# Layer 0 of a two-layer block: the first granule finished and normalized once, and the q/k/v epilogues begun one by one behind their last sums

## The chip, the core and the metric

One Trainium2 chip, one of its cores. The metric is the device time of one execution in microseconds (us). Engines are named as in the profile: PE is TensorE, DVE is VectorE, ACT is ScalarE, POOL is GpSimd, and SP is the queue that issues most DMAs. Each engine works off its own instructions strictly in the order in which the program wrote them; a waiting instruction holds up all that stand behind it on its engine.

## The reference

Two layers on x of 256 tokens by 2048 features, all in float32. Each layer computes six adaLN vectors from the condition c, a mixer (layer 0: differential attention; layer 1: an SSD scan) and a SwiGLU. What bears on the change is the start of layer 0:

```python
ada = silu(c) @ ada_w[0] + ada_b[0]              # shift1, scale1, gate1, shift2, scale2, gate2
h = rms_norm(x, norm1_g[0]) * (1.0 + scale1) + shift1
q, k, v = split(h @ da_w_in)                     # 2048 columns each: 16 heads of 2 x 64 (v: 128)
q = partial_rope(rms_norm(q, q_norm_g)); k = partial_rope(rms_norm(k, k_norm_g))
a = softmax(q0 k0) - lam * softmax(q1 k1)        # causal, two softmaxes for each head
x = x + gate1 * (rms_norm(a @ v, subln_g) * (1 - lambda_init)) @ w_out
```

## The kernel before

**Matrix products.** Weights arrive by DMA in units of 256 rows by 512 columns (a tile `raw`, one of 7). ACT rounds a unit to the fast format (`wh`, the "cast" of line 253), DVE makes the rest (`wl` = raw - wh), and PE multiplies three times (high by high, high by low, low by high): 12 matmuls of 512 columns for one unit and 256 tokens. At most four units are split ahead of their products (`W_BUFS`), so the cast of a unit is written into ACT's queue when the products of the fourth unit before it are written into PE's. A unit's `wl` is written one unit later than its cast.

**Order.** The program is one stream: units go into a list (`fifo`) together with plain calls (`call(fn)`), and are popped from it in turn. Popping writes instructions into the engines' queues. Generators in `active` (epilogues, attention blocks) are advanced one step after each popped unit (`step_all`, by `tick`).

**Granules.** shift1 and scale1 are needed before h exists, and their weights (`ada_first`, tiles `araw`, 9 buffers) have to be loaded as well. So the start is cut into eight granules g of 256 features. `push_mods(g)` multiplies the eight `araw` units of a granule in pairs ("adaLN pairs", 8 matmuls of 32 output rows, tile `po` or `wk`); `finishes[g]` turns the sums into columns T0 and S0 (four small matmuls `wk<-c,adasb` on PE, three short DVE operations T, S, S); `normed(g)` makes h of the granule (`hm`, then `ah` and `al`). Then `push_early(n, g)` multiplies this granule with six chunks of 512 columns, n = 0 to 5. By their names in `keys` they are q0, k0, v0, q1, k1, v1 (the q, k and v columns of head groups 0 and 1). Its `collect` copies (g = 0, ACT) or adds (g > 0, DVE) the two PSUM banks of the unit to an SBUF pair `part[n]`, called `partoh` (even n) and `partol` (odd n) in the profile. There are four such banks (`mm`), so the second unit after one waits for that one's sum.

The function `item(i, g)` places the work of granule g-1 among the eight `araw` units i of granule g. For g = 1 it finishes and normalizes granule 0 at i = 0, before its first products; and the two branches `elif i == 1` and `elif i == 2`, which hold for every g from 1 on, do both a second time for g = 1.

**Epilogues.** After the sums of granule 7, `complete(n, ...)` starts the end of a chunk: v is copied (line 989), q and k run `epilogue`, at most three at a time (`EPI`): squares on ACT (924), sums of 64 on DVE (`qss`), 1/sqrt on POOL (388, 389: one pair for each half b of the tokens), 16 scalings of 64 columns on ACT (937), the rotation on POOL and DVE, transposes on PE into a `wk` bank (three of these), and ACT's evacuation of each bank to `qT` or `kT` (959). Attention blocks (`attend`) of a head group start when its q and k are done: products of q and k on PE (`wk<-negm,identb`, then `wk<-kT,qT`), maxima on DVE, exponentials on ACT (1031), the combination of the two softmaxes on DVE (tile `e`), transposes of e on PE, their copy on ACT, products with v.

**The chunks after.** From n = 6 on (q2, k2, ...) each chunk is one product over all 2048 rows, 8 units in a row in one pair of `mm` banks; the first six epilogues and the first attention blocks run beside chunk 6. Adds of adaLN rows (`acc`) for later stages run on DVE in between.

Of the kernel before, what the change touches and what calls it, by code (L numbers as in the profile page):

```python
# [90 lines left out]
def block_kernel(ctx: ExitStack, tc: tile.TileContext, x, x_t, columns_in, ssd_columns, da_columns, ada_w, ada_b,  # L91
# [85 lines left out]
    def step_all():  # L177
        for g in list(active):
            if next(g, StopIteration) is StopIteration:
                active.remove(g)  # L180
        gap["n"] -= 1
        if pending and gap["n"] <= 0 and pending[0][0]():
            _, g, n = pending.popleft()
            gap["n"] = n
            if next(g, StopIteration) is not StopIteration:
                active.append(g)
# [40 lines left out]
    def pop():  # L227
        kind, fn = fifo.popleft()
        if kind == "c":
            fn()  # L230
            return
        if waiting["u"] <= 1:
            low_parts()
        done = fn()
        waiting[kind] -= 1 if done is None else done
        if kind == "u":
            tick()

    def flush():
        low_parts()  # L240
        while fifo:
            pop()

    def call(fn):
        fifo.append(("c", fn))
# [17 lines left out]
    def push_unit(w, row, col, n, mm):  # L263
        while waiting["u"] >= limit["u"]:
            pop()
        u = split_unit(w, row, col, n)
        waiting["u"] += 1
        fifo.append(("u", lambda: mm(u)))
# [10 lines left out]
    def products(ps, hl, half, w, n, first, last):  # L279
        h, l = hl  # L280
        wh, wl = w
        for a in range(2):
            k = 2 * half + a
            pe.matmul(ps[:, :n], h[:, k, :], wh[:, a, :n], start=first and a == 0, stop=False)
            pe.matmul(ps[:, :n], h[:, k, :], wl[:, a, :n], start=False, stop=False)
            pe.matmul(ps[:, :n], l[:, k, :], wh[:, a, :n], start=False, stop=last and a == 1)
# [458 lines left out]
    def small_loads():  # L745
        sp.dma_start(da_cols, da_columns[:, 0:36])
        sp.dma_start(lv, da_columns[:, 36:292].rearrange("p (i d) -> p i d", i=4))
# [75 lines left out]
    def push_mods(g, item):  # L823

        st = {}
        sl = slice(2 * g, 2 * g + 2)

        def use(raw, u):
            if u == 0:
                st["ps"] = bank(("po", "wk")[g % 2])  # L830
            if u % 2 == 0:
                st["raw"] = raw
                return
            for k in range(2 * u - 2, 2 * u + 2):
                t = k % 4
                pe.matmul(st["ps"][32 * t:32 * t + 32, :], cT32[:, k, :], (st["raw"], raw)[t // 2][:, k % 2, :],
                          start=(k < 4), stop=(k >= 12), tile_position=(0, 32 * t), skip_group_check=True)
            if u == 7:
                st["sb"] = tmp("adasb")
                act.copy(st["sb"], st["ps"])  # L840

        def finish():
            ps2 = bank("wk")
            for i in range(4):
                pe.matmul(ps2[:, i:i + 1], st["sb"][:, i * 128:(i + 1) * 128], c32, start=True, stop=True)
            dve.tensor_tensor(T0[:, sl], ps2[:, 0:2], b_cols[0, 0][:, sl], op=ALU.add)
            dve.tensor_tensor(S0[:, sl], ps2[:, 2:4], b_cols[0, 1][:, sl], op=ALU.add)
            dve.scalar_tensor_tensor(S0[:, sl], S0[:, sl], 1.0, n1c[0][:, sl], op0=ALU.add, op1=ALU.mult)
        for u in range(8):
            item(u)  # L850
            push_raw(ada_first, u * 256, g * 512, lambda raw, u=u: use(raw, u), first)
        return finish
# [39 lines left out]
    def scale_quarter(q):  # L892
        v = x_quarter(q).rearrange("p (k t) -> p k t", k=4)
        dve.tensor_tensor(v, v, held["rps"][:, None, 0:256].to_broadcast([128, 4, 256]), op=ALU.mult)
# [18 lines left out]
    n_early = N_EARLY  # L913
    part = {}
# [50 lines left out]
    def complete(n, src, in_psum):  # L965

        hg, i = keys[n]
        nm = ("q", "k", "v")[i]

        def ahead():  # L970
            return hg >= 2 and (begun, ended)[i == 2][hg - 2] < 3
        if in_psum:
            while ahead():
                step_all()
            if i < 2:
                tiles = []
                for b in range(2):
                    t = held["dp"].tile([128, 512], F32, tag="qn", name="qn", bufs=2)
                    act.copy(t, src[b])
                    tiles.append(t)  # L980
                src = tiles

        def steps(src=src):
            while ahead():
                yield
            if i == 2:
                v = held["dp"].tile([128, 2, 512], F32, tag="v", name="v", bufs=2)
                for b in range(2):
                    act.copy(v[:, b, :], src[b])
                ready[n] = v  # L990
            else:
                dst = held["dp"].tile([128, 4, 256], F32, tag=f"{nm}T", name=f"{nm}T", bufs=2)
                yield from epilogue(nm, dst, n, src)
        g = steps()
        if next(g, StopIteration) is not StopIteration:
            active.append(g)
# [117 lines left out]
    def push_early(n, g):  # L1114

        hg, i = keys[n]
        q, half = g // 2, g % 2
        bk = Banks()

        def run(u):  # L1120
            for b in range(2):
                products(bk()[b], norm_a.h[q][b], half, u, 512, True, True)
        push_unit(wi, g * 256, i * D + hg * 512, 512, run)

        def collect():
            if g == 0:
                tg = ("oh", "ol")[n % 2]
                part[n] = [op_.tile([128, 4, 128], F32, tag=tg, name=f"part{tg}")
                           .rearrange("p a n -> p (a n)") for b in range(2)]
            for b in range(2):  # L1130
                if g == 0:
                    act.copy(part[n][b], bk()[b])
                else:
                    dve.tensor_tensor(part[n][b], part[n][b], bk()[b], op=ALU.add)
        call(collect)

    ada_job(0, 2, fin_gate("m0", True), gate=True)
# [16 lines left out]
    def normed(g):  # L1154
        norm_pair(g)
        done.append(g)

    def item(i, g):
        if g == 0:
            if i in (2, 6):  # L1160
                call(token_rstd if i == 2 else scale_tokens)
            return
        at["p"] += 1
        first = 0 if g == 1 else 3
        if g == 1 and i == 0:
            flush()
            for fn in (finishes[0], low_parts, lambda: normed(0)):
                call(fn)
            push_early(0, 0)
            small_loads()  # L1170
            dve.tensor_copy(identb, ident)
        elif i == 1:
            call(finishes[g - 1])
        elif i == 2:
            call(lambda: normed(g - 1))
        if g == 1 and i in (3, 5, 7):
            call(lambda: scale_quarter(i // 2))
        if i == first:
            while g - 1 not in done:
                pop()  # L1180
            todo.extend((n, g - 1) for n in range(1 if g == 1 else 0, n_early))
            lead = 2 if g == 1 else 0
            span.update({"from": at["p"] - lead, "to": at["p"] + 8 - lead, "n": len(todo)})
        while todo and len(todo) * (span["to"] - span["from"]) > span["n"] * (span["to"] - at["p"]):
            push_early(*todo.popleft())

    for g in range(8):
        if g == 2:
            call(lambda: active.append(rotary_tables()))
        if g == 4:  # L1190
            call(lambda: ada.update(rate=1.5, metered=METER))
        finishes.append(push_mods(g, lambda i, g=g: item(i, g)))
    for k in range(max(3, len(todo))):
        if k == 1:
            call(finishes[7])
        elif k == 2:
            call(lambda: norm_pair(7))
            call(open_dp)
        if todo:
            push_early(*todo.popleft())  # L1200
    call(lambda: ada.update(rate=0.0, acc=0.0))
    for n in range(n_early):
        push_early(n, 7)
    call(lambda: [complete(n, part[n], False) for n in range(n_early)])
    call(lambda: ada.update(rate=DA_RATE, metered=METER))

    def load_x():
# [3 lines left out]
    for n in range(n_early, 12):  # L1211
        if n == n_early + 1:
            call(load_x)
        hg, i = keys[n]
# [649 lines left out]
```

## Time and profile before

| | |
|---|---|
| time, median of 3 runs | 2683.26 us (2683.25 to 2684.19) |
| the profiled execution | 2684.56 us, of which the trace's span is 2682.8 us |
| PE busy | 2637.8 us (98% of the span) |
| DVE busy | 1956.5 us (73%) |
| ACT busy | 1373.9 us (51%) |
| DMA | mean 255 GB/s |

The profile is of one execution. Times in its rows count from the start of the span. Shares over the whole span are averages over stages; what the changed lines are worth is read from the first 300 us, where they work.

### The profile page before, as it was taken

How to read it: one execution, taken by the hardware profiler on the slowest of the kernel's cores; microseconds unless marked ns; L12 is line 12 of the kernel's file. 1: busy time of each engine (PE TensorE's matmuls, PEld its weight loads, DVE VectorE, ACT ScalarE, POOL GpSimd, SP SyncE). 2: the span in 40 equal slices, each digit the busy share in tenths (PEclk: the TensorE clock that was granted, in tenths of full speed). 3: DMA queues.
4: the chain of work that ended last, by engine and by line, in shares of the span. 5: the costliest groups of instructions: out<-in, count | busy, mean ns of one | idle time of the engine just before them, and what ended most of it. 6: DMA issues, size and time to landing. Idle time of an engine off the chain costs nothing.

```text
span 2682.8 us, 35840 instructions
## 1 busy us (share of the span) xinstructions
PE 2637.8 (98%) x13224; PEld 2191.7 (82%) x13224; DVE 1956.5 (73%) x2240; ACT 1373.9 (51%) x2037; POOL 197.7 (7%) x205
## 2 busy tenths in 40 slices
PE   7997999999999999999999999999999999999999
PEld 4665887888888888888999989988888888888887
DVE  4876887777888876777777777786677554446776
ACT  4336775545444444446546566565545444444443
POOL 0003331000111210001000010000000000000001
PEclk9998999999999999999999999999999999999999
DMA  8985787698889887885566666666687655556885
GB/s 348 373 308 194 255 282 291 233 346 305 308 310 345 317 316 254 287 290 179 169 229 227 214 233 234 206 234 193 201 316 287 191 185 188 193 188 229 284 287 184
DMA packets 193136, 685.09 MB, mean 255 GB/s; under 512 B 22224, under 2 KB 30784, under 8 KB 191680
## 3 DMA queue, kind: packets, MB, share of 16 engines
q1 hardware_dynamic: 191232, 680.93, 72.4%
q8 instruction: 104, 1.70, 0.3%
q0 software_dynamic: 864, 1.62, 0.2%
q14 instruction: 72, 0.59, 0.1%
q10 hardware_dynamic: 864, 0.24, 0.0%
HBM read 680.52 MB, written 2.19 MB: 254 GB/s over the span
## 4 chain that ended last, share of the span: by engine, by line
PE 94%; DVE 2%; ACT 2%; DMA 1%; issue 1%; POOL 1%; SPq 0%; DVEq 0%; ACTq 0%; POOLq 0%
PE mm L118 75%; PE wk L118 15%; PE po L118 4%; DMA araw<-in_ada_w 1%; DVE wl L118 1%; ACT wh L253 0%; POOL qr L389 0%; DMA raw<-in_da_w_in 0%; DVE res L118 0%; DVE x L118 0%; ACT partol L937 0%; ACT e L1031 0%; DVE acc L118 0%; DVE partol L118 0%; ACT hm L554 0%
## 5 line engine op out<-in xcount | busy, mean ns | idle before, releaser
L253 ACT CAST wh<-raw 128x1024 fp32r<-128x1024 f32 (+1 forms) x888 | 924.5, 1046 | 1071.4 <-PE mm L118 776.9
L118 DVE TENSOR_TENSOR wl<-raw,wh 128x1024 fp32r<-128x1024 f32 (+1 forms) x888 | 1104.4, 1253 | 442.0 <-ACT wh L253 438.6
L118 PE MATMUL mm<-wh,ah 128*128 128x512 f32 (+1 forms) x2560 | 1017.9, 398 | 8.0 <-ACT ah L907 3.8
L118 PE MATMUL mm<-wl,ah 128*128 128x512 f32 (+1 forms) x2560 | 1000.0, 391 | 4.0 <-DVE wl L118 4.0
L118 PE MATMUL mm<-wh,al 128*128 128x512 f32 (+1 forms) x2560 | 1000.3, 391 | 0.0
L118 PEld LDWEIGHTS mm<-wh,ah 128*128 128x128 f32 x2560 | 482.6, 189 | 131.2 <-issue 18.7
L118 PEld LDWEIGHTS mm<-wl,ah 128*128 128x128 f32 x2560 | 483.0, 189 | 104.1 <-DVE wl L118 7.1
L118 PEld LDWEIGHTS mm<-wh,al 128*128 128x128 f32 x2560 | 482.3, 188 | 103.3 <-DVE al L118 1.9
L118 DVE SCALAR_TENSOR_TENSOR acc<-raw,cT,acc 128x1024 f32<-128x1024 f32 x300 | 383.4, 1278 | 0.3
L118 PE MATMUL wk<-wl,ah 128*128 128x512 f32 x360 | 140.2, 389 | 0.0
L118 PE MATMUL wk<-wh,ah 128*128 128x512 f32 x360 | 140.1, 389 | 0.0
L118 PE MATMUL wk<-wh,al 128*128 128x512 f32 x360 | 140.0, 389 | 0.0
L118 PE MATMUL mm<-ah,wh 128*128 128x256 f32 x720 | 118.8, 285 | 0.0
L118 PE MATMUL mm<-al,wh 128*128 128x256 f32 x720 | 117.7, 283 | 0.0
L118 PE MATMUL mm<-ah,wl 128*128 128x256 f32 x720 | 117.6, 283 | 0.0
L508 POOL PARTITION_ALL_REDUCE gate<-acc x12 | 41.2, 3477 | 943.2 <-DVE acc L118 936.4
L118 PEld LDWEIGHTS mm<-ah,wh 128*128 128x128 f32 x720 | 100.2, 192 | 0.1
L118 PEld LDWEIGHTS mm<-ah,wl 128*128 128x128 f32 x720 | 100.2, 192 | 0.0
L118 PEld LDWEIGHTS mm<-al,wh 128*128 128x128 f32 x720 | 100.2, 192 | 0.0
L118 PEld LDWEIGHTS wk<-wl,ah 128*128 128x128 f32 x360 | 67.5, 188 | 14.2 <-DVE wl L118 0.4
L118 PEld LDWEIGHTS wk<-wh,al 128*128 128x128 f32 x360 | 67.6, 188 | 14.1
L118 PEld LDWEIGHTS wk<-wh,ah 128*128 128x128 f32 x360 | 67.6, 188 | 14.1
(305 smaller groups left out, 2047.8 us busy)
## 6 DMA issues: line engine op xcount, KB each, us to landing
raw<-in_ffn_w_gate_up SPq DMA_DIRECT2D x352, 512.0 KB, 4.6
raw<-in_ada_w SPq DMA_DIRECT2D x320, 512.0 KB, 5.1
raw<-in_ffn_w_down SPq DMA_DIRECT2D x176, 512.0 KB, 4.8
raw<-in_ssd_w_in SPq DMA_DIRECT2D x136, 512.0 KB, 4.5
raw<-in_da_w_in SPq DMA_DIRECT2D x96, 512.0 KB, 5.3
araw<-in_ada_w SPq DMA_DIRECT2D x64, 512.0 KB, 8.4
raw<-in_ssd_w_out SPq DMA_DIRECT2D x64, 512.0 KB, 4.3
raw<-in_da_w_out SPq DMA_DIRECT2D x32, 512.0 KB, 5.4
```

The source lines that it names most:

```text
L118: return fn(dst, *a, **k)
L253: act.copy(wh[:, :, :n], raw[:, :, :n])
L508: pool.partition_all_reduce(mods["G", key][:, o:o + 512], acc[:, i * 512:(i + 1) * 512], 128, ReduceOp.add)
```

## The change

`item` leaves out the second finish and the second normalization of granule 0. `complete` is no longer called for all six chunks in one go behind the last sum of granule 7, but for each chunk behind its own last sum.

```diff
@@ push_early, collect @@
                     act.copy(part[n][b], bk()[b])
                 else:
                     dve.tensor_tensor(part[n][b], part[n][b], bk()[b], op=ALU.add)
+            if g == 7:
+                complete(n, part[n], False)
         call(collect)
@@ item @@
-        elif i == 1:
+        elif i == 1 and g > 1:
             call(finishes[g - 1])
-        elif i == 2:
+        elif i == 2 and g > 1:
             call(lambda: normed(g - 1))
@@ behind the granules @@
     for n in range(n_early):
         push_early(n, 7)
-    call(lambda: [complete(n, part[n], False) for n in range(n_early)])
     call(lambda: ada.update(rate=DA_RATE, metered=METER))
```

How the queues change is shown at three places. The first is PE's queue behind the third of granule 0's six products (36 matmuls `mm`), a piece of the difference, where `wk<-c,adasb` are the small matmuls of the finish and `wk<-araw,cT` is the first adaLN pair of granule 1:

```order
 L118 MATMUL mm<-wl,ah 128x512
 L118 MATMUL mm<-wh,al 128x512
-L118 MATMUL wk<-c_96,adasb 128x1 x4
 L118 MATMUL wk<-araw,cT_115 32x512 x4
 L118 MATMUL mm<-wh,ah 128x512
```

The four small matmuls are gone; on ACT and DVE the second `hm`, `ah` and T, S, S, `al` are gone in the same way, and everything else stands in the same order there.

The second place is ACT's queue from the casts behind the last normalization (granule 7) on. Before, the third of these seven casts is that of v1's last unit, and the seventh that of the fourth unit of chunk 6:

```order
L253 CAST wh<-raw 128x1024 x7
L924 ACTIVATE sq<-partoh 128x512 x2
L924 ACTIVATE sq<-partol 128x512 x2
L989 COPY v<-partoh 128x512 x2
L924 ACTIVATE sq<-partol 128x512 x2
L989 COPY v<-partol 128x512 x2
L253 CAST wh<-raw 128x1024 x2
L937 ACTIVATE partoh<-partoh,qr 128x64 x8
L937 ACTIVATE partol<-partol,qr 128x64 x16
L253 CAST wh<-raw 128x1024
L937 ACTIVATE partoh<-partoh,qr 128x64 x8
L937 ACTIVATE partol<-partol,qr 128x64 x16
```

and now, in the same queue from the same place:

```order
L253 CAST wh<-raw 128x1024 x2
L924 ACTIVATE sq<-partoh 128x512 x2
L253 CAST wh<-raw 128x1024
L924 ACTIVATE sq<-partol 128x512 x2
L253 CAST wh<-raw 128x1024
L989 COPY v<-partoh 128x512 x2
L937 ACTIVATE partoh<-partoh,qr 128x64 x8
L253 CAST wh<-raw 128x1024
L924 ACTIVATE sq<-partol 128x512 x2
L937 ACTIVATE partoh<-partoh,qr 128x64 x8
L937 ACTIVATE partol<-partol,qr 128x64 x8
L253 CAST wh<-raw 128x1024
```

The squares, copies and scalings, which stood in blocks behind the seventh cast, now stand between the casts from the third one on.

The third place is DVE's queue at the sums of granule 7 (`partoh<-partoh,mm` and `partol<-partol,mm`, two instructions for each chunk). Before, from q0's sum on:

```order
L118 TENSOR_TENSOR partoh<-partoh,mm 128x512 x2
L118 SCALAR_TENSOR_TENSOR acc<-raw,cT,acc 128x1024
L118 TENSOR_TENSOR wl<-raw,wh 128x1024
L118 TENSOR_TENSOR partol<-partol,mm 128x512 x2
L118 TENSOR_TENSOR wl<-raw,wh 128x1024
L118 TENSOR_TENSOR partoh<-partoh,mm 128x512 x2
```

and now, from the same sum on:

```order
L118 TENSOR_TENSOR partoh<-partoh,mm 128x512 x2
L118 SCALAR_TENSOR_TENSOR acc<-raw,cT,acc 128x1024
L118 TENSOR_REDUCE qss<-sq 128x8 x2
L118 TENSOR_TENSOR wl<-raw,wh 128x1024
L118 TENSOR_TENSOR partol<-partol,mm 128x512 x2
L118 TENSOR_REDUCE qss<-sq 128x8 x2
L118 TENSOR_TENSOR wl<-raw,wh 128x1024
L118 TENSOR_TENSOR partoh<-partoh,mm 128x512 x2
```

The reductions of q0, k0 and q1, which stood together behind v1's sum, now stand behind each chunk's own sum and in front of the sums that follow. On PE the first transposes of q0 move from behind the seventh unit of chunk 6 to behind its second, the first product of q and k from behind its eighth to behind its fifth, and from the first unit of chunk 7 on all queues hold the same order as before.

## Rows read from the trace of the kernel before

**Rows 1.** A view of the page: TensorE's granted clock in 40 equal slices of the span (tenths of its upper level), and the chain of work that ended last, by engine.

```profile
PEclk9998999999999999999999999999999999999999
...
PE 94%; DVE 2%; ACT 2%; DMA 1%; issue 1%; POOL 1%; SPq 0%; DVEq 0%; ACTq 0%; POOLq 0%
```

**Rows 2.** A view of the busy time in stretches of 20 us; the columns are the busy time (and instructions) of PE, weight loads, DVE, ACT and POOL, then TensorE's granted clock as a share of its upper level, the DMA share and GB/s.

```profile
220.00:240.00 20.00, 13.69 (x52) 10.38 (x51) 8.88 (x11) 15.94 (x53) 10.18 (x12) 0.86 0.52 170
240.00:260.00 20.00, 13.00 (x62) 9.50 (x63) 12.68 (x25) 12.68 (x40) 6.60 (x14) 0.67 0.71 277
260.00:280.00 20.00, 18.06 (x88) 13.46 (x85) 14.21 (x27) 16.14 (x53) 7.25 (x11) 0.87 0.35 106
280.00:300.00 20.00, 20.00 (x116) 16.07 (x114) 15.86 (x24) 15.11 (x46) 8.51 (x9) 1.00 0.76 251
```

**Rows 3.** A view of the waits of TensorE in the first 500 us: who waited for whom, us in total, times, longest.

```profile
PE wk L118 <- DVE e L118: 5.4, 1, 5.4
PE wk L118 <- DVE partoh L118: 5.0, 2, 4.2
```

**Rows 4.** A view of TensorE's timeline around the end of the first granule's first products (start us, us, engine, line, operation, [idle before, and what ended it]).

```profile
35.48 0.94 PE L118 MATMUL wk<-c,adasb 128*128 128x1 f32 x8
36.36 1.07 PE L118 MATMUL wk<-araw,cT 128*32 128x512 f32 x8
38.90 0.50 PE L118 MATMUL mm<-wh,ah 128*128 128x512 f32 x1 [1.48 <-ACT ah L907]
```

**Rows 5.** A view of the busy time in stretches of 5 us, same columns as rows 2.

```profile
40.00:45.00 5.00, 5.00 (x26) 3.87 (x28) 4.10 (x4) 1.80 (x4) 0.00 (x0) 1.00 0.29 118
50.00:55.00 5.00, 3.63 (x32) 1.38 (x24) 0.61 (x4) 2.55 (x5) 0.00 (x0) 1.00 0.94 363
```

**Rows 6.** A view of VectorE's timeline from the last granule's sums to the first rotations.

```profile
199.56 1.27 DVE L118 TENSOR_TENSOR partoh<-partoh,mm 128x512 f32<-128x512 f32 x2
203.09 1.27 DVE L118 TENSOR_TENSOR partol<-partol,mm 128x512 f32<-128x512 f32 x2
...
210.09 1.28 DVE L118 TENSOR_TENSOR partoh<-partoh,mm 128x512 f32<-128x512 f32 x2
...
214.01 2.46 DVE L118 TENSOR_REDUCE qss<-sq 128x8 f32<-128x512 f32 x4 [0.32 <-ACT sq L924]
...
230.00 1.23 DVE L118 TENSOR_TENSOR wl<-raw,wh 128x1024 fp32r<-128x1024 f32 x1 [6.80 <-ACT wh L253]
...
236.68 1.23 DVE L118 TENSOR_TENSOR wl<-raw,wh 128x1024 fp32r<-128x1024 f32 x1 [4.26 <-ACT wh L253]
```

**Rows 7.** A view of ScalarE's groups of instructions between 198 and 262 us (count | busy us, mean ns | idle before, and what ended it).

```profile
L253 ACT CAST wh<-raw 128x1024 fp32r<-128x1024 f32 x13 | 13.3, 1046 | 17.7 <-PE mm L118 14.7 <-DVE partol L118 2.9
...
L1031 ACT ACTIVATE e<-wk,mx 128x128 f32<-128x128 f32 x8 | 2.8, 376 | 1.4 <-DVE mx L118 1.4
```

**Rows 8.** A view of ScalarE's timeline in that stretch.

```profile
213.35 1.15 ACT L924 ACTIVATE sq<-partoh 128x512 f32<-128x512 f32 x2
...
227.01 2.02 ACT L937 ACTIVATE partol<-partol,qr 128x64 f32<-128x64 f32 x8 [2.60 <-POOL qr L389]
...
231.80 3.92 ACT L937 ACTIVATE partol<-partol,qr 128x64 f32<-128x64 f32 x16
235.62 2.92 ACT L253 CAST wh<-raw 128x1024 fp32r<-128x1024 f32 x3
```

**Rows 9.** A view of TensorE's timeline in the same stretch.

```profile
203.91 0.47 PE L118 MATMUL mm<-wh,ah 128*128 128x512 f32 x1 [0.56 <-DVE partol L118]
...
209.47 0.39 PE L118 MATMUL mm<-wh,ah 128*128 128x512 f32 x1
...
212.19 0.39 PE L118 MATMUL mm<-wh,ah 128*128 128x512 f32 x1
...
230.02 0.49 PE L118 MATMUL mm<-wh,ah 128*128 128x512 f32 x1 [1.35 <-ACT wh L253]
231.28 0.79 PE L118 MATMUL mm<-wl,ah 128*128 128x512 f32 x1 [0.77 <-DVE wl L118]
231.87 0.63 PE L118 MATMUL mm<-wh,al 128*128 128x512 f32 x1
232.30 0.63 PE L118 MATMUL mm<-wh,ah 128*128 128x512 f32 x1
...
239.77 1.09 PE L118 MATMUL wk<-ident,partoh 128*128 128x128 f32 x4 [4.20 <-DVE partoh L118]
...
250.48 0.39 PE L118 MATMUL wk<-negm,identb 128*128 128x512 bf16 x1 [0.41 <-ACT qT L959]
...
257.94 1.17 PE L118 MATMUL wk<-ident,e 128*128 128x128 f32 x4 [5.42 <-DVE e L118]
...
269.19 0.50 PE L118 MATMUL mm<-wh,ah 128*128 128x512 f32 x1
```

**Rows 10.** A view of VectorE (first row) and GpSimd (the others) where they work side by side.

```profile
218.34 3.67 DVE L118 TENSOR_TENSOR wl<-raw,wh 128x1024 fp32r<-128x1024 f32 x3
...
217.08 1.64 POOL L389 TENSOR_TENSOR qr<-qr,neghalf 128x8 f32<-128x8 f32 x1
218.80 0.80 POOL L388 TENSOR_SCALAR qr<-qss 128x8 f32<-128x8 f32 x1
219.69 2.67 POOL L389 TENSOR_TENSOR qr<-qr,neghalf 128x8 f32<-128x8 f32 x1
```

## The prediction

> **What bounds the kernel now.** I read the page first: TensorE carries 94% of the chain that ended last, and its granted clock is at the upper of its two levels in nearly every slice [rows 1]. So a change pays only where PE stands still or runs slowly, and what is won there stays won if PE is the bound afterwards. The stretches of 20 us show such a place: between 220 and 280 us PE is busy 13.69, 13.00 and 18.06 us of 20 at a granted clock of 0.86, 0.67 and 0.87; from 280 us on it is busy 20.00 of 20 at 1.00, with DMA at 0.76 [rows 2]. That hole is where the first six epilogues and the first attention blocks run. PE's waits name its two longest stops: 4.2 us for the rotated q0 (`partoh`) and 5.4 us for the combined softmax `e` [rows 3]. A second, small place is PE's timeline at 36 to 39 us [rows 4].
>
> **Second finish of granule 0, removed.** Behind 36 matmuls PE runs the four small matmuls from 35.48 to 36.36 (0.88 us), then an adaLN pair, about 1.0 us, and then stands until 38.90 for `ah`, which ACT is making a second time: 1.54 us [rows 4]. The cast and `wl` of the next two units are ready by then (they stand ahead of the removed instructions on ACT and DVE), and the adaLN pairs of granule 1 keep their places, so the unit of 38.90 can start behind the pair at 36.5: 2.4 us earlier. Does the gain last? In the 5 us after 40 the DMA share is 0.29, so what was asked for had landed and the next transfers waited for PE to free buffers; from 50 us on DMA is at 0.94 and more [rows 5]. The transfers are thus released by PE and move with it. I take 2.4 us; the bounds are 0 (a later transfer sets the pace and does not move) and 2.6 (a little more behind `al`).
>
> **Epilogues one by one: what the hole is made of.** Before, ACT does the squares and copies in one block from 213.35, then waits 2.60 us for POOL's 1/sqrt, then runs scalings in long runs (3.92 us from 231.80 for 16), and the casts of the next units stand behind: three at 235.62 [rows 8]. DVE waits for those casts 6.80 and 4.26 us, with the rotations of q0 queued behind its `wl` [rows 6]; PE runs out of units at 228.7 (1.35 us before 230.02), stops again before 231.28, then 4.20 us before q0's transposes, reaches the first product of q and k at 250.48 and the transposes of e at 257.94, and starts chunk 7 only at 269.19 [rows 9]. From there on the order is unchanged, so I measure the change by when PE gets to that place.
>
> I walk the new queues by hand, on the clock of before, leaving the 2.4 us out. Steps from start to start: a sum of two banks 1.2 (1.27 less overlap), a `wl` or `acc` about 1.15, two reductions 1.2 [rows 6]; a cast 0.96, two squares 1.05, eight scalings 1.95 [rows 7, 8]; a unit on PE 2.72 (209.47 to 212.19) [rows 9]. A unit starts about 0.8 after the sum that frees its bank (203.09 to 203.91) [rows 6, 9].
>
> *To the end of the sums.* q0's sum is at 199.56 as before. ACT squares it until 201.4, DVE reduces 202.0 to 203.2, so `wl` and then k0's sum slip from 203.09 to 204.3. Squares of k0 until 206.2, reductions until 206.9, `wl`, v0's sum at 208.0. q1's at 210.3. ACT is then busy with v0's copies, q0's first scalings and a cast, so q1's squares end at 213.8, its reductions at 214.5, `wl` at 215.6, and k1's sum, at 210.09 before [rows 6], starts at 215.6. Chunk 6's first unit needs that bank: 216.4 instead of 212.19 [rows 9]. Here the change costs PE 4.2 us.
>
> *To the first product of q and k.* ACT now has no block: scalings of q0 and k0, a cast (218.7), scalings of k0, a cast (221.6), v1, scalings of q1 with a cast between (225.6) and behind (228.5), q0's first evacuation, a cast (230.1), q0's and k0's evacuations, k1's squares, a cast (233.4), k0's last evacuation at 234.0. v1's sum ends at 221.0, q0's rotation at 222.1 (its POOL part waits for nothing: the six 1/sqrt end by 218). PE does units 1 to 5 of chunk 6 with the transposes between them until 233 (or 234 where the clock is low, without effect) and then waits for k0 at 234.0. Before, that product stood at 250.48: 16.4 us earlier, with three units still to do.
>
> *To chunk 7.* Product until 235.1; DVE reaches the maxima behind two `wl`, two `acc` and k1's reductions at 237.7; exponentials until 241.2 (2.75 us), combination until 243.0. PE fills this with the three units, 8.2 us, and q1's transposes, until 243.8, and transposes e without a wait: 14.1 earlier than 257.94. Next product until 246.0. Then ACT: its queue holds casts and k1's 16 scalings ahead of the copy of e, which ends at 249.1; PE waits 3.1 us. Products with v, k1's transposes, the second combination (253.0), its transposes, k1's evacuations at 254.0, third product, chunk 7 at 255.5. That is 13.7 us earlier. I take 2.2 off, since behind such waits PE starts at the lower of its two levels (1.2 instead of 2.4 GHz): after the 1.35 and 0.77 us before 231.28 matmuls follow each other at 0.43 us (231.87 to 232.30) where a unit at full rate has 2.72 / 12 = 0.23 [rows 9]; eight such matmuls are 1.6 us, and another 0.6 is my allowance for the short ones. **11.5 us.**
>
> The cover of it: ACT has about 46.5 us of work between 200 and chunk 7 (13 casts, 64 scalings, 16 squares and copies of v, 8 evacuations, exponentials), and the walk leaves it 8 us of waits. Bounds for this edit: if PE never waited there, 12 units at 2.72 and about 10 us of transposes and attention products from 200.3 would bring it to chunk 7 at 243: a gain of 26. At the other end the 4.2 us are lost and nothing is won back: -4.2.
>
> One resource gets busier at once: POOL's 1/sqrt now runs beside DVE's sums and `wl`. Before, where they met, a 0.20 us POOL instruction took 0.80 and one of 1.64 took 2.67, while three `wl` took 3.67 instead of some 3.5 [rows 10]: POOL pays, DVE hardly. POOL's results have 4 us and more to spare in the walk, so I add nothing. The Trainium skill, SBUF — State Buffer, section "SBUF: two separate sides", says that a VectorE operation with two SBUF inputs and a GpSimd operation hold a shared port for a whole instruction, and whichever starts first blocks the other. By this DVE would also be the loser at times: four `wl` of the walk, each up to 1.64 behind a 1/sqrt, would make the sums up to 6.6 us later, and the time 2676. The trace agrees on POOL's side, not on DVE's.
>
> **Sum.** 2.4 + 11.5 = 13.9. The profiled execution took 2684.56 (a span of 2682.8 and 1.76 around it); it lies 1.3 above the median of 2683.26. Against the median: 2683.26 - 13.9 = **2669.4 us**.
>
> **Rivals.** *A, ACT and DVE in lockstep.* Each reduction waits for squares that wait for a sum, and DVE holds `wl` and sums behind it; if POOL or hand-overs cost more than the walk grants, the units of chunk 6 starve too. DVE blocked by POOL is one form of it, with 0.06 of its 0.24: four `wl` behind 1.64 us each make 6.6, so 2683.3 - (13.9 - 6.6) = 2676. For it speaks that DVE is full from 199 to 213 [rows 6]; against it that POOL's results have slack. At half of the gain, 5.7 + 2.4 = 8: 2675. *B, no change to speak of*: the attention chain e is bound by ACT's later work, so the earlier q and k only make it wait elsewhere; gain under 5.4: about 2680. Against it: ACT was idle 17.7 us before casts in this stretch [rows 7]. *C, slower*: only the delay of the sums is real. The first unit of chunk 6 comes 4.2 us late, and casts behind scalings keep it so: each of units 5 to 8 then waits for its cast. It decides from the point where a cast comes later than PE's unit; in the walk the margins are 2 to 5 us, so some 3 us more on ACT in each would be needed. With four waits of 2 us: 4.2 + 8 - 2.4 = +10, 2693. *D, better*: PE's second half runs without the half clock and without the 3.1 us: a gain of 19, 2664.
>
> **Chances.** Forecast (gain 10 to 17) 0.5, D 0.12, A 0.24, B 0.1, C 0.04. What a measurement here can tell from no change is 0.2%, 5.4 us. Faster 0.86, same 0.1, slower 0.04. The range leaves out B and C below and the gains beyond 23: 2660 to 2678.
>
> **What would show it.** In the profile after: PE's wait for `ah` near 37 us gone and reductions `qss` between the sums; chunk 6 starting some 2 us later than before (4.2 - 2.4); the first `wk<-negm` near 232 instead of 250.5; no wait of PE for `partoh` of 4 us; chunk 7 near 255 instead of 269.2; then PE full, and all later places earlier by the same 14 us. Wrong would be: casts or `wl` late for units 3 to 8 of chunk 6; a clock under 0.8 over 210 to 255; or a lead at chunk 7 that shrinks later, which would mean that a transfer and not PE sets the pace there.

## The result and the profile after

The changed kernel took 2666.91 us (median of 6 runs, 2666.38 to 2670.05) against 2683.26 of before in the same rounds: a ratio of 0.9942 with a 95% interval of 0.9929 to 0.9954, 16.35 us less by the medians. The forecast was 2669.4 us, in a range of 2660 to 2678. The profiled execution took 2667.55 us at a span of 2665.8, 17.0 us less than the span before. One execution of one kernel in the experiments took 3455.28 us at a granted clock of 0.711 throughout, against 0.997 and more in its other five, and is left out of that kernel's median.

The page of after, TensorE's granted clock in 40 slices and the chain that ended last:

```profile
PEclk9999999999999999999999999999999999999999
...
PE 93%; DVE 2%; ACT 1%; DMA 1%; issue 1%; POOL 0%; SPq 0%; DVEq 0%; ACTq 0%; POOLq 0%
```

The bound is the same as before [rows 1]; only what PE lost inside has become less. The stretches of 20 us that answer to [rows 2], same columns; the first row is that of before from 200 to 220 us, the others are those of after:

```profile
200.00:220.00 20.00, 19.14 (x83) 15.52 (x84) 18.93 (x26) 11.64 (x17) 4.80 (x6) 1.00 0.62 207
...
200.00:220.00 20.00, 15.73 (x60) 12.29 (x61) 16.41 (x25) 17.05 (x49) 15.59 (x18) 0.91 0.47 153
220.00:240.00 20.00, 20.00 (x112) 16.34 (x111) 17.55 (x30) 16.88 (x47) 6.22 (x10) 1.00 0.73 245
240.00:260.00 20.00, 16.85 (x91) 12.90 (x89) 15.20 (x28) 17.47 (x55) 8.14 (x13) 0.91 0.75 279
260.00:280.00 20.00, 20.00 (x109) 16.13 (x108) 16.36 (x25) 16.22 (x52) 7.19 (x8) 1.00 0.73 236
```

The hole that was 13.69, 13.00 and 18.06 us of 20 is now 20.00, 16.85 and 20.00. From 200 to 220 us, where the sums are, PE is busy less than before: 15.73 us against 19.14. PE's waits between 190 and 290 us:

```profile
PE mm L118 <- DVE partoh L118: 3.3, 3, 2.0
PE po L118 <- ACT e L1054: 2.4, 1, 2.4
PE mm L118 <- DVE partol L118: 2.1, 2, 1.8
PE wk L118 <- ACT kT L959: 0.6, 2, 0.3
```

The two long waits of [rows 3], 5.4 us for `e` and 4.2 for the rotated q0, are gone. What is left is waits for the sums (up to 2.0) and one for the copy of `e` (2.4).

PE's timeline of after, at the places of [rows 4] and [rows 9]:

```profile
35.66 1.06 PE L118 MATMUL wk<-araw,cT 128*32 128x512 f32 x8
36.65 0.50 PE L118 MATMUL mm<-wh,ah 128*128 128x512 f32 x1
...
212.96 0.47 PE L118 MATMUL mm<-wh,ah 128*128 128x512 f32 x1 [1.98 <-DVE partoh L118]
...
230.58 0.59 PE L118 MATMUL wk<-negm,identb 128*128 128x512 bf16 x2
...
241.01 0.60 PE L118 MATMUL wk<-ident,e 128*128 128x128 f32 x4
...
245.32 2.08 PE L118 MATMUL po<-v,e 128*128 128x128 f32 x8 [2.43 <-ACT e L1054]
247.19 1.54 PE L118 MATMUL wk<-ident,partoh 128*128 128x128 f32 x8
248.86 0.74 PE L118 MATMUL wk<-ident,e 128*128 128x128 f32 x4
...
251.73 0.50 PE L118 MATMUL mm<-wh,ah 128*128 128x512 f32 x1
```

ACT's copy of `e`, for which PE waits 2.43 us:

```profile
244.66 0.61 ACT L1054 COPY e<-wk 128x512 f32<-128x512 f32 x1
```

The unit behind the first pair starts at 36.65 instead of 38.90 and waits for nothing. Further on all of PE's work is 3.6 us earlier (q0's sum on DVE: 195.96, before 199.56). The first product of q and k stands at 230.58 (before 250.48), the transposes of `e` at 241.01 (257.94), chunk 7 at 251.73 (269.19), 17.46 us earlier. Of these 3.6 came with the lead and 13.9 were won between q0's sum and chunk 7. From there PE has no wait of more than 0.1 us until 290 us; where the kernel before stands at 281 us the lead is 17.5, at the end 17.0.

### The profile page after: what moved, and what is told of

It reads as the page before. It is cut to its first block, busy times and chain, and to the rows that moved or that the text cites. A ratio compares the mean times of both kernels' runs of the same rounds, so it can differ in the third digit from the quotient of the medians.

```text
span 2665.8 us, 35822 instructions
## 1 busy us (share of the span) xinstructions
PE 2629.3 (99%) x13216; PEld 2186.7 (82%) x13216; DVE 1955.4 (73%) x2236; ACT 1371.6 (51%) x2034; POOL 200.7 (8%) x205
## 4 chain that ended last, share of the span: by engine, by line
PE 93%; DVE 2%; ACT 1%; DMA 1%; issue 1%; POOL 0%; SPq 0%; DVEq 0%; ACTq 0%; POOLq 0%
PE mm L118 74%; PE wk L118 15%; PE po L118 4%; DVE wl L118 1%; DMA araw<-in_ada_w 1%; DMA raw<-in_da_w_in 0%; ACT wh L253 0%; DMA raw<-in_ssd_w_in 0%; DVE acc L118 0%; ACT e L1031 0%; DVE res L118 0%; DVE x L118 0%; DMA x<-in_x_t 0%; ACT hm L554 0%; DVE hm L118 0%
## 5 line engine op out<-in xcount | busy, mean ns | idle before, releaser
L118 PEld LDWEIGHTS wk<-wh,al 128*128 128x128 f32 x360 | 67.6, 188 | 13.9
```

The lines of the kernel that those rows point to most:

```text
L118: return fn(dst, *a, **k)
```

## The experiments

Medians are set against those of before in the same rounds (2682.75 to 2683.4). As a second measure that single executions give, I read the stretch from the start of q0's sum on DVE to the end of the first unit of chunk 7 on PE: 72.50 us before, 58.62 after. How far such stretches carry is told at the end of this section.

**Each edit alone.** One run leaves out only the second finish and normalization, the other only brings the epilogues one by one.

```diff
 # finish once only (kernel before, plus)
-        elif i == 1:
+        elif i == 1 and g > 1:
             call(finishes[g - 1])
-        elif i == 2:
+        elif i == 2 and g > 1:
             call(lambda: normed(g - 1))
```

> Only the second finish and normalization of granule 0 are left out; the epilogues still start all at once. Theory 1 (the two edits are independent and the transfers move with PE): 2.4 to 3.6 us faster, 2680 us; the adaLN pair that stood at 64.0 us is near 60. Theory 2 (the second edit needs the first, or the early lead is lost to a transfer later): 0 to 1 us. On the clock: the changed kernel is 2.5 us ahead at 52 us and 4.05 at 64, because behind the same two waits (1.39 and 0.76) its matmuls did not fall to the lower clock level. If the removed idle time at 37 us is what saves the clock there, this run shows 4.05 at 64 too; if it was chance, 2.5.

> Only the epilogues are started one by one; granule 0 is finished and normalized twice as before. Theory 1: 13 to 14 us faster, 2669.5 us, and chunk 7 begins near 255.3 (269.19 less 13.9). Theory 2 (each edit needs the other): under 10 us. On the clock: matmuls near 57 us at the lower level (0.43 us apart) as in the kernel before.

Measured: finish once 2679.05 us (2678.19 to 2682.29), a ratio of 0.9986 with 0.9977 to 0.9994, 4.35 us less. Epilogues one by one 2671.51 (2671.18 to 2672.22), 0.9956 with 0.9943 to 0.9968, 11.9 less. Together 16.25, against 16.35 for the whole: the two add up, and neither needs the other. As sizes, the first lies above the 2.4 to 3.6 forecast and the second below the 13 to 14, but the intervals (1.6 to 6.2 and 8.6 to 15.3) hold both forecasts. With the finish alone, the waits of 5.4 and 4.2 us stand as before; with the epilogues alone they are gone, and the stretch is 58.64.

Where could 4.35 us come from, when the removed wait and small matmuls are 2.4? PE's rows around the next stop show one source. Before:

```profile
55.75 0.50 PE L118 MATMUL mm<-wh,ah 128*128 128x512 f32 x1 [1.39 <-ACT wh L253]
57.01 0.79 PE L118 MATMUL mm<-wl,ah 128*128 128x512 f32 x1 [0.76 <-DVE wl L118]
57.60 0.63 PE L118 MATMUL mm<-wh,al 128*128 128x512 f32 x1
58.03 0.63 PE L118 MATMUL mm<-wh,ah 128*128 128x512 f32 x1
...
64.01 1.06 PE L118 MATMUL po<-araw,cT 128*32 128x512 f32 x8
```

After:

```profile
53.22 0.50 PE L118 MATMUL mm<-wh,ah 128*128 128x512 f32 x1 [1.39 <-ACT wh L253]
54.48 0.50 PE L118 MATMUL mm<-wl,ah 128*128 128x512 f32 x1 [0.76 <-DVE wl L118]
54.82 0.40 PE L118 MATMUL mm<-wh,al 128*128 128x512 f32 x1
55.06 0.40 PE L118 MATMUL mm<-wh,ah 128*128 128x512 f32 x1
...
59.96 1.06 PE L118 MATMUL po<-araw,cT 128*32 128x512 f32 x8
```

The two stops are the same, 1.39 and 0.76 us. Before, the matmuls behind them follow each other at 0.43 us, the lower level of the clock; after, at 0.24. The lead grows there from 2.53 to 4.05. The run with the finish alone has the fast form (granted clock 1.00 in 50 to 60), the run with the epilogues alone the slow one (0.90). A stop of 0.73 us for `adasb`, at 51.45 before and 48.93 after, is there in both.

Does the fast form come from the removal of the second finish, which took away the stop of 1.48 us at 37? Eleven traces of this case are of kernels without the second finish, with the same program up to q0's last sum. Ten have the fast form (1.00 in 50 to 60), but one has the slow one (0.83): the run with later sums and all scalings on DVE, told below, which has no stop between 36 and 48 us either:

```profile
53.51 0.50 PE L118 MATMUL mm<-wh,ah 128*128 128x512 f32 x1 [1.39 <-ACT wh L253]
54.77 0.79 PE L118 MATMUL mm<-wl,ah 128*128 128x512 f32 x1 [0.76 <-DVE wl L118]
55.36 0.63 PE L118 MATMUL mm<-wh,al 128*128 128x512 f32 x1
```

So the earlier stop alone does not decide it; why the clock falls there in one execution and not in another stays open. The lead at q0's sum shows the scatter: it is 2.2 to 5.0 us in these eleven traces (median 4.2), each against the one trace of before. The 2.2 is that of the run with the slow form, close to the forecast. Part of the scatter stands ahead of the change: the granted clock from 20 to 30 us is 0.66 to 0.70 in five of them (leads 2.2 to 3.9) and in before, and 0.83 in six (leads 4.2 to 5.0).

**Which chunks count.** Two kernels keep the finish once, but bring only some chunks early; the others' epilogues begin together behind the last sum.

```diff
 # q0 and k0 early (changed kernel, plus); the counterpart has (2, 3, 5) and (0, 1, 4)
-            if g == 7:
+            if g == 7 and n in (0, 1):
                 complete(n, part[n], False)
...
         push_early(n, 7)
+    call(lambda: [complete(n, part[n], False) for n in (2, 3, 4, 5)])
```

> The changed kernel, but only q0 and k0 are begun behind their own sums; v0, q1, k1 and v1 are begun together behind the last sum. Theory chain (the gain is that the first product of q and k comes while product units are left to stand between it and the transposes of e): the order keeps that (two units between), so at least 11 of the 13.9 us stay: 2667 to 2670 us. Theory block (the gain is that the squares, copies and scalings no longer stand in one block in front of chunk 6's casts): much of the block is back behind the last sum, half of the gain is lost: 2673 to 2676 us.

> The changed kernel, but only v0, q1 and v1 are begun behind their own sums; q0, k0 and k1 are begun behind the last sum. ACT's work is as spread out as in e3, but the first product of q and k stands behind all eight units of chunk 6 again, with no unit between it and the transposes of e. Theory chain: the second edit wins 5 us at most, 2675 to 2680 us, with PE waits of about 5 us for e and for q0 or k0. Theory block: most of the gain stays, 2668 to 2672 us.

Measured: q0 and k0 early 2667.0 us (2665.57 to 2668.35), 16.4 less: as good as all six. v0, q1 and v1 early: 2673.62 (2672.0 to 2674.57), 9.8 less, of which the finish has 4.35, so 5.4 are left of the 11.9. PE's longest waits between 190 and 290 us of the first and of the second:

```profile
PE wk L118 <- ACT qT L959: 4.5, 2, 3.2
```

```profile
PE wk L118 <- DVE e L118: 6.5, 2, 5.2
PE wk L118 <- DVE partol L118: 3.8, 2, 2.8
```

The whole of the gain comes with q0 and k0: the first product stands early enough for chunk 6's units to cover the exponentials. Without them PE waits for `e` again. But 2673.62 lies between the two forecasts of that run (2675 to 2680 and 2668 to 2672), and 5.4 us are more than nothing: breaking up ACT's block seems to be worth something without q0 and k0. The intervals of a few us don't tell 5.4 from the "at most 5" of the chain theory. In the run with q0 and k0 early the wait moves to q1's evacuations (3.2 us at 243) and takes the place of the one for the copy of `e`.

**What is left: late sums, ACT or DVE?** After the change PE still stands 8.4 us between 190 and 290. One kernel calls each epilogue one sum later, one moves all early scalings from ACT to DVE (8 instructions of 0.68 to 0.81 us instead of 64 with a pace of 1.95 us per 8), one only those of q1 and k1.

```diff
 # one sum later
-            if g == 7:
-                complete(n, part[n], False)
+            if g == 7 and n > 0:
+                complete(n - 1, part[n - 1], False)
...
         push_early(n, 7)
+    call(lambda: complete(n_early - 1, part[n_early - 1], False))
...
 # scalings on DVE: n < 6; the third kernel has n in (3, 4)
         for b in range(2):
-            for g in range(8):
-                act.mul(q3[b][:, g, :], q3[b][:, g, :], rs[b][:, g:g + 1])
+            if n < 6:
+                dve.tensor_tensor(q3[b], q3[b], rs[b][:, :, None].to_broadcast([128, 8, 64]), op=ALU.mult)
+            else:
+                for g in range(8):
+                    act.mul(q3[b][:, g, :], q3[b][:, g, :], rs[b][:, g:g + 1])
```

> As the changed kernel, but each chunk's epilogue is called one sum later (q0's behind k0's sum, and so on; k1's behind v1's sum, v1's at the end). Chain theory: the first unit of chunk 6 comes less late, since only two pairs of reductions stand ahead of k1's sum instead of three and they wait for no squares (about 2 us instead of 4.4), but q0 and k0 are ready one sum, 3 to 4.7 us, later, and PE then waits for them or for e: the two are nearly even, 2666 to 2669, against 2666.9 of the changed kernel. Rival, lockstep (the sums that wait for squares cost the 4.4 us outright and the attention chain has slack): chunk 6 earlier by 2.4 and nothing lost, 2664 to 2665.

> As the changed kernel, but the 64 scalings of the early chunks (ACT, 16 per chunk, 1.95 us for 8 from start to start) are 8 broadcast multiplications on DVE (estimate from a sum of the same shape: 0.68 us each, 5.5 in all). ACT loses 15.6 us of the 55 between 196 and 251. Theory: up to 217 us DVE sets the pace and later the chain through ACT does, so the copy of e no longer waits behind scalings (2.4 us back), while the sums slip a little more: 2663 to 2667. Rival, ACT is the bound all through 205 to 250 (the changed kernel still has 7 us of idle PE there, and some 2 at half clock): at least 6 us back, 2661 or less. Rival, DVE is the bound: its 5.5 us more come on top, 2669 to 2672.

> As the changed kernel, but only the scalings of q1 and k1 (the later two) are on DVE; those of q0 and k0 stay on ACT. Theory: the units of chunk 6 start as late as in the changed kernel (nothing moves before 213 us), and the copy of e (PE's 2.43 us wait at 245) is no longer behind k1's scalings: 2 us back, 2664 to 2666. Rival ACT bound: 2663 or less. Rival DVE bound: 2668 to 2670.

Measured: 2667.47, 2667.29 and 2667.36 us, 15.3 to 15.5 less than before, all three within the scatter of the changed kernel. That speaks against the rivals (late sums outright; ACT the bound, 6 us back; DVE the bound, 2 to 5 us lost). But my theory isn't borne out either. It had 2 us back with all scalings on DVE (2663 to 2667) and with those of q1 and k1 alone (2664 to 2666), and both came out above. With one sum later the time is as forecast (2666 to 2669), but not for the reason given: q0 and k0 were to be ready later, and the first product in fact stands 1.8 us earlier behind q0's sum. Parts did get earlier. With each epilogue one sum later, chunk 6's first unit comes 1.6 us late instead of 4.4 and the transposes of `e` 3.3 us earlier after q0's sum; with all scalings on DVE the copy of `e` holds nobody up. PE gives it back, as its rows of the run with all scalings on DVE show:

```profile
244.02 0.66 PE L118 MATMUL wk<-ident,partoh 128*128 128x128 f32 x4 [1.76 <-ACT e L1034]
246.00 0.74 PE L118 MATMUL wk<-ident,e 128*128 128x128 f32 x4 [1.32 <-ACT osq L1083]
...
249.91 0.79 PE L118 MATMUL mm<-wh,ah 128*128 128x512 f32 x1
250.51 0.63 PE L118 MATMUL mm<-wl,ah 128*128 128x512 f32 x1
```

The 2.43 us wait has become two of 1.76 and 1.32, and chunk 7 begins at the lower clock: its first unit takes 4.6 us (249.91 to 254.54), where that of after takes 2.85 (251.73 to 254.58). The stretch is 59.40 us, 60.13 with one sum later and 60.31 with q1 and k1 alone, against 58.62.

**POOL beside DVE.** The changed kernel with one more 1/sqrt behind those of q0, k0 and q1, so that POOL has no gap.

```diff
             rs.append(rstd_of(ss, 8, 64, "qr"))
+        if n in (0, 1, 3):
+            rstd_of(ss, 8, 64, "qr2")
```

> As the changed kernel, but POOL does one more 1/sqrt (0.20 and 1.64 us alone) behind the pairs of q0, k0 and q1, whose result nobody reads, so that POOL works without a gap beside DVE's sums, reductions and wl from 199 to about 217 us. Theory (POOL pays for the overlap): wl, acc, reductions and sums of DVE stay within 0.15 us of their lengths, the first unit of chunk 6 starts within 0.5 us, and the time is 2666 to 2669 (a later rotation of q0 by up to 2 us is the only cost). Rival (a DVE instruction also stands still behind a POOL instruction that began first): three more of 1.64 us, so sums up to 4.9 later and a time of 2670 to 2672, with single wl or acc of 2 us and more in the rows.

Measured: 2668.83 us (2666.93 to 2669.75), 13.9 less than before and within the forecast (2666 to 2669). VectorE's rows, then GpSimd's, of this run:

```profile
199.71 1.22 DVE L118 TENSOR_TENSOR wl<-raw,wh 128x1024 fp32r<-128x1024 f32 x1
...
202.23 1.34 DVE L118 TENSOR_REDUCE qss<-sq 128x8 f32<-128x512 f32 x2
203.49 1.22 DVE L118 TENSOR_TENSOR wl<-raw,wh 128x1024 fp32r<-128x1024 f32 x1
...
211.18 1.21 DVE L118 TENSOR_TENSOR wl<-raw,wh 128x1024 fp32r<-128x1024 f32 x1
212.31 1.28 DVE L118 TENSOR_TENSOR partoh<-partoh,mm 128x512 f32<-128x512 f32 x2
...
220.87 0.39 DVE L118 TENSOR_TENSOR partoh<-partoh,Aq 128x128 f32<-128x128 f32 x1 [3.18 <-POOL rt L946]
```

```profile
199.58 1.65 POOL L389 TENSOR_TENSOR qr<-qr,neghalf 128x8 f32<-128x8 f32 x1
...
203.59 2.61 POOL L389 TENSOR_TENSOR qr<-qr,neghalf 128x8 f32<-128x8 f32 x1
206.28 0.81 POOL L388 TENSOR_SCALAR qr<-qss 128x8 f32<-128x8 f32 x1
...
211.18 2.71 POOL L389 TENSOR_TENSOR qr<-qr,neghalf 128x8 f32<-128x8 f32 x1
```

POOL's instructions stretch from 1.64 to 2.61 and 2.71 and from 0.20 to 0.81 where a `wl` began before them or within 0.01 us of them; DVE's stay at 1.21 to 1.34. The sums start where they did (k1's 16.2 us behind q0's, both here and in after). The cost is another: q0's rotation waits 3.18 us for POOL's results, where I had said up to 2, and the stretch is 61.41 us against 58.62. The median lies 1.9 us above that of the changed kernel, with ranges that overlap.

The Trainium skill, SBUF — State Buffer, section "SBUF: two separate sides", says of a VectorE instruction with two SBUF inputs, as `wl` is, that whichever of the two engines starts first blocks the other. The trace agrees where POOL is the later one. It doesn't where POOL began first: the `wl` of 199.71 began 0.13 us behind a POOL instruction and that of 215.27 1.02 us behind another, and they took 1.22 and 1.23 us, as they do elsewhere.

**Filling a stop.** The changed kernel with 16 transposes that nobody reads, ahead of the first products with v, where PE waited 2.43 us.

```diff
         po = pos[hg, qb]
+        if (hg, qb) == (0, 0):
+            for _ in range(16):
+                pe.transpose(po[:, 0:128], ident, ident)
```

> The changed kernel with 16 transposes of the identity (nobody reads them; about 0.11 us each at full rate, 1.8 us) in PE's queue right ahead of the first products with v, where PE stands 2.43 us for the copy of e. Theory (PE's standing still is what lowers the clock behind it): the products with v take 1.1 us instead of 2.08 and the transposes behind them 1.2 instead of 1.54, at a granted clock of 1.00; the time moves by 1 us at most (2665.5 to 2667.5), since the next transposes of e then wait for DVE or ACT. Rival (the clock falls for the whole stretch whatever PE does at this one place): the products still take 2.08 us.

Measured: 2666.98 us (2666.09 to 2669.42). PE's rows:

```profile
241.43 1.97 PE L118 MATMUL po<-ident 128*128 128x128 f32 x16
243.90 1.16 PE L118 MATMUL po<-v,e 128*128 128x128 f32 x8 [0.51 <-ACT e L1054]
244.90 1.22 PE L118 MATMUL wk<-ident,partoh 128*128 128x128 f32 x8
247.44 0.74 PE L118 MATMUL wk<-ident,e 128*128 128x128 f32 x4 [1.32 <-ACT osq L1083]
...
250.98 0.79 PE L118 MATMUL mm<-wh,ah 128*128 128x512 f32 x1
251.58 0.63 PE L118 MATMUL mm<-wl,ah 128*128 128x512 f32 x1
```

The time is as forecast, and so are the lengths behind the filled stop: the products with v take 1.16 us instead of 2.08 and the transposes 1.22 instead of 1.54. But that the filling did it is not shown. In the run with more work on POOL, which fills nothing, PE stood 2.22 us at the same place, and the same work ran at the upper level too:

```profile
246.74 1.16 PE L118 MATMUL po<-v,e 128*128 128x128 f32 x8 [2.22 <-ACT e L1056]
247.74 1.23 PE L118 MATMUL wk<-ident,partoh 128*128 128x128 f32 x8
```

So behind nearly the same stop the clock fell in one execution and not in another. What both runs show is that the fall isn't gone: some 5 us later, behind a stop of 1.32 us, the lower level comes, and chunk 7's first unit takes 3.8 us with the filled stop and 3.4 with more work on POOL, instead of 2.85. With the filled stop the total stays.

**Two combinations.** Each epilogue one sum later with all scalings on DVE, and q0 and k0 early with the scalings of q1 and k1 on DVE. The second was run twice, and its rows are from the second time.

> Each epilogue one sum later and all early scalings on DVE: the early part without the 4.4 us that the sums lost, and ACT without 15.6 us of scalings. Theory as before (stops move, the first unit of chunk 7 runs at half clock): 2665 to 2668. Rival (the two losses, late sums and a full ACT, are independent and each hid the gain of removing the other): 5 us or more back, 2662 or less.

> q0 and k0 finished early as in the run with these two alone, v0, q1, v1 and k1 behind the last sum, and the scalings of q1 and k1 on DVE instead of ACT (7.8 us off ACT). That run waited 4.5 us for q1's evacuations at 238 to 243. Theory (what a stop gives back reappears as another stop or as a start of chunk 7 at half clock, since PE has too few product units for the whole chain up to chunk 7): 2665.5 to 2668, with chunk 7 starting at most 2 us earlier after q0's sum than the changed kernel's 55.8 us, or its first unit longer than 2.85 us. Rival (ACT's scalings are what is left to win): 4 us back, 2663 or less.

> The same kernel as the run with q0 and k0 early and q1 and k1 scaled on DVE, for its rows (that run left a profile at a clock of 0.711 throughout, which tells nothing of this change). It measured a ratio of 0.9932. If the gain over the changed kernel is real, the ratio comes out at 0.9925 to 0.9940 again, and the first unit of chunk 7 ends 1 to 3 us earlier after q0's sum than in the changed kernel (58.62 us there). If it was scatter, the ratio is 0.994 or more, and that unit ends within 0.7 us of 58.6.

Measured: later sums with DVE 2666.71 us (2663.72 to 2668.3), 16.2 less; the stretch is 57.01 us. The two losses are not independent gains of 5 us. The time is in the range of the theory (2665 to 2668), but its sign is not there: the first unit of chunk 7 takes 2.85 us, at the upper level, and PE has stopped 2.32 us for `e` before. q0 and k0 early with q1 and k1 on DVE: 2664.4 us (median of five, 2663.92 to 2666.11), a ratio of 0.9932 with 0.9919 to 0.9946, and 2664.97 (2664.56 to 2666.18), 0.9934 with 0.9920 to 0.9947. The stretch is 57.45 us, 1.2 shorter than after. The first time lies below the range of the theory (2665.5 to 2668) and above that of the rival (2663 or less); the second repeats it, with a ratio and a stretch as the gain would have them. Both medians lie below all runs of the changed kernel, so this is the best version found, by some 2 us (0.07%). But the intervals overlap by more than that, and the two were not run side by side, so a gain over the changed kernel is likely and not shown. The wait of 4.5 us for q1's evacuations has become 0.79, and in its place stand the stops of 1.76 and 1.32 and a first unit of chunk 7 of 3.7 us (248.56 to 252.24), as in the runs above.

How much the stretch tells: with the finish alone it is 70.64 us, against 72.50 before, with the same order of work in it. The rows show the clock behind it: chunk 6's last unit takes 4.9 us before (243.67 to 248.59, granted clock 0.50 in 244 to 248) and 3.4 with the finish alone (239.78 to 243.18, 0.88 in 240 to 244), and neither the code nor the stops ahead of it differ there. Differences of 2 us between single stretches thus prove nothing.

## Why the prediction was right, and where its terms were off

- **The bound.** Right: PE's hole between 220 and 280 us was worth time, and what was won there stayed (17.5 us of lead at 281, 17.0 at the end).
- **Second finish, 2.4 us with bounds 0 and 2.6: right in its mechanism, probably too small.** The wait for `ah` went as forecast and the next unit came 2.25 us earlier. At 50 us the lead was 2.53. But in the trace of after the stretch at half clock at 57 us was gone too, and the lead settled at 3.6; timed alone it gave 4.35, with an interval (1.6 to 6.2) that still holds 2.4. In ten of eleven traces the lead at q0's sum is above the upper bound of 2.6; the eleventh, with the half clock at 55 us, has 2.2. How much of the excess belongs to the removed finish and how much to chance in the clock stays open. My step "the transfers move with PE, so the lead stays" looked for a loss only; the clock behind a later stop was not among the terms.
- **Sums one by one.** The walk had the first unit of chunk 6 4.2 us late; it was 4.37 late once the lead of 3.6 is taken off. k0's and v0's sums stood at 200.68 and 204.44, which is 204.3 and 208.0 on before's clock, the walked times.
- **The first product, the transposes, chunk 7.** Walked to 234.0, 243.8 and 255.5; with 3.6 added, the trace has 234.2, 244.6 and 255.3. The wait for the copy of `e`, walked at 3.1, was 2.43. Of the walk's cover of ACT's work, 46.5 us, some 2 us are a miscount: it has 16 squares and copies of v, and the queue holds 12; no term of the sum uses it. One agreement is luck: the walk has PE wait for k0's last evacuation at 234.0, but that ended at 229.92 (233.5 with 3.6 added), and PE came to the product later, without a wait.
- **The allowance of 2.2 us for the half clock, taken off the walk: the mis-sized term.** The half clock came, at 214 to 217 and at 245 to 248 us (0.60 in 244 to 248). It cost little, since both times it lay ahead of a wait: for ACT's copy of `e`, and for the bank of the next transposes of `e`. For the first, DVE took the maxima only at 233.96, 1.7 us behind the end of the products, and the copy of `e` ended at 245.27, which is 248.9 on before's clock; the walk had 249.1. For the second, the runs with the filled stop and with more work on POOL had no half clock there and stand 1.32 us in its place: in all three the next transposes of `e` start 3.5 us behind the start of the products with v (245.32 to 248.86 in after). So edit 2 of the sum, 11.5, came out at 13.9 in the trace; timed alone it gave 11.9, with an interval (8.6 to 15.3) that holds both. The profiled execution of before lies 1.3 us above its median, which is part of the gap. The timed 11.9 alone would not have told 11.5 from 13.7; that the allowance was not needed rests on the traces.
- **The sum.** 13.9 against 16.35: by these readings 1.2 to 2 from the finish, the rest from the allowance. A split of 2.45 us is finer than the scatter of single traces, so it is an estimate.
- **Rivals.** B and C fell with the result. A, lockstep, is real as the 4.4 us at chunk 6 and no more: calling each epilogue one sum later removes 2.8 of it and leaves the time as it was. Its form with DVE blocked by POOL did not show: in after and in the run with more work on POOL no `wl` between 195 and 226 us took more than 1.35 us, and those that began behind a 1/sqrt took 1.21 to 1.23. D was half right: the half clock did not cost, but the wait for `e` stayed.
- **What I had not seen.** The chain behind the walk has little to spare on any side: six of seven other orders or divisions of the same work end within 2.5 us of the changed kernel (the seventh, without q0 and k0 early, loses 6.7). In their rows a stop that is removed comes back as another stop or as a unit at half clock.

## What to carry to other kernels

Walk the queues by hand to the place from which the order is unchanged, and measure the change there: this gave 255.5 where the trace had 255.3. Subtract a half clock only where no wait follows that absorbs it. Don't put a half clock that comes or goes down to an edit by one trace: here the same stops were followed by either level in kernels with the same code up to that place, and the lead of one edit came out between 2.2 and 5.0 us. When several repairs of the same hole give the same time, moving pieces of the chain between engines pays little (2 us at best here). I take it that what is short then is work to cover the chain with; no run here tests that by adding such work.

## What the runs showed of the hardware

- The same two stops (1.39 and 0.76 us) were followed by matmuls 0.43 us apart or 0.24 apart. With a stop of 1.48 us some 18 us ahead of them the lower level came in both traces; without it, in one trace of eleven.
- Behind a stop of 2.43 us the products with v took 2.08 us, behind one of 2.22 at the same place 1.16, and behind the stop filled with 16 transposes of 0.12 us also 1.16. In the last two the lower level came some 5 us later, behind a stop of 1.32 us.
- Beside DVE's `wl`, a GpSimd instruction of 1.64 us took up to 2.71 and one of 0.20 took 0.81, where `wl` had begun first or at the same time. Where a GpSimd instruction of 1.64 us had begun first (0.13 to 1.02 us), neither was slower: 1.64 or 1.65 us, and 1.21 to 1.23 for `wl`.
